# A transformer block on one core: gate and head stores issued by ScalarE, gate loads issued by POOL, and SiLU written as a product with Sigmoid

## The chip, the cores and the metric

The kernel runs on one core of a Trainium2 chip. The core's engines run their own instruction streams and wait for each other through semaphores: TensorE (PE in the profile; PEld are its weight loads), VectorE (DVE), ScalarE (ACT), GpSimd (POOL) and SyncE (SP, which only issues DMA transfers here). ScalarE and POOL can issue transfers too; each engine's instructions, its transfer issues among them, go in program order. The metric is the device time of one execution in microseconds, lower being better.

## The reference

One layer of a block over 512 latent tokens and 256 context tokens, D = 1024, all fp32. Cut to what the change touches:

```python
h_lat = rms_norm(x, norm_mix_g) * (1.0 + sc1) + sh1              # (512, 1024)
(qkv, ..., g_a, ..., g_b, m_a, m_b) = split_last(h_lat @ w_in, IN_SIZES)
# g_a, g_b: 512 wide (4 heads of 128); m_a, m_b: 1024 wide

def gated_head_norm(o, g, gate, dtype):                           # o: output of a scan, per head
    o = o * lax.rsqrt(jnp.mean(o * o, axis=-1, keepdims=True) + EPS) * g
    return (from_heads(o) * jax.nn.silu(gate)).astype(dtype)

ya = gated_head_norm(oa, gdn_g, g_a, dtype) @ w_up_a              # branch A: gated DeltaNet
yb = gated_head_norm(ob, hgrn_g, g_b, dtype) @ w_up_b             # branch B: HGRN2
mix = (jax.nn.sigmoid(m_a) * ya + jax.nn.sigmoid(m_b) * yb) @ w_out
x = x + g1 * mix
x = x + g2 * swiglu(rms_norm(x, norm_ffn_g) * (1.0 + sc2) + sh2, ffn_w_in, ffn_w_out)
out = rms_norm(x, final_norm_g)
```

## The kernel before

Activations lie transposed: 128 features on the partitions, 512 tokens along them. A matmul in fp32 precision is made of three: each operand is split into a high part (`hi`, a cast on ScalarE, L100) and a low part (`lo`, a subtraction on VectorE, L102), and `mm3` (L110) adds hi·hi, hi·lo and lo·hi. Weights come as `raw` tiles on SyncE's queue (L92).

The stages follow each other roughly so: modulation and norm of the input (to 60 us), the first gates (60 to 85 us), the projections and scans of the two branches (85 to 580 us), the join of both branches with their up-projections (580 to 645 us), the output projection, and the feed-forward part (from 690 us).

*Gates.* 24 rows of gate columns of `w_in`, each 128 x 512: numbers 0 to 3 are `g_a`, 4 to 7 `g_b`, 8 to 15 `m_a`, 16 to 23 `m_b`. `gate_out` copies one from PSUM (`pg` for the first six, `pgate` after) into a tile `gt` of a ring of two, and stores it to the scratch tensor `gdram` in DRAM. The first eight are 16 to 23, in that order; 0 to 15 are worked in as filler among the scans, the last ones just ahead of the join.

*Heads.* `head_norm` takes one head's scan output: squares (L427), a mean (L429 or L431 on VectorE), a power on POOL (L432), a scaling on ScalarE into `on` (L434), a transpose on TensorE into `pt` (L437), and a copy `y` (L438), which is stored to `ydram`. Names with `p0` to `p3` are pairs of DeltaNet heads' state, `h0` to `h3` HGRN2 heads.

*Join.* `branch(br)` loads for each of its four heads the gate `ug` and the head `uy` back from DRAM, makes SiLU of the gate, multiplies, and splits the product into `yh` and `yl`. `up(br, W, ys)` then makes eight up-projections `pup`, in two PSUM banks in turn; each is evicted by VectorE with its merge gate `mg`, on which ScalarE has made Sigmoid. For branch 0 the eviction writes into `mt`, a view of the tile `x1` (printed as `x`); for branch 1 it adds up.

*Modulation.* In the background POOL loads pieces of `mod_w` (`mwb`, L833, and `mwe`, L847), and VectorE sums them (`acc`, L835; L851 to L854).

The order of instructions on each engine is set by a scheduler, by priorities and estimated durations of its own. A table `PLAN` sets the order in which the scans' steps are written, a priority raised by 5000 puts the last gates and the modulation behind. The engine that issues a transfer is the one on whose `nc.` name it is called: `nc.sync`, `nc.scalar`, `nc.gpsimd`.

Of the kernel before, what the change touches and what calls it, by code (L numbers as in the profile page):

```python
# [7 lines left out]
F32 = mybir.dt.float32  # L8
F32R = mybir.dt.float32r
U8 = mybir.dt.uint8  # L10
AF = mybir.ActivationFunctionType
ALU = mybir.AluOpType

P = 128
# [3 lines left out]
SEQ = 512  # L18
# [30 lines left out]
def body(tc, T, out, tap=None):  # L49
    nc = tc.nc  # L50
# [7 lines left out]
    with ExitStack() as root:  # L58
# [17 lines left out]
        def bank(tag, name):  # L76
            return ps_.tile([P, 512], F32, name=name, tag=tag, bufs=BANKS[tag])

        def pmm(name):
            return bank("mm", name)  # L80
# [48 lines left out]
        gdram = dr.tile([24, P, SEQ], F32, name="gdram")  # L129
        ydram = dr.tile([8, P, SEQ], F32, name="ydram")  # L130
# [3 lines left out]
        def gate_out(i, ps, pool, tag="raw"):  # L134
            gt = pool.tile([P, SEQ], F32, name=f"gt{i}", tag=tag, bufs=2)
            nc.scalar.copy(gt[:, :], ps[:, :])
            nc.sync.dma_start(gdram[i, :, :], gt[:, :])

        def gate(i, pool, wpool=None, tag="mm"):
            gate_out(i, feat(split([W_IN[:, gcols[i]:gcols[i] + P]], KT, P, wpool), lat, SEQ, f"pgate{i}", tag=tag), pool, "gt")  # L140
# [18 lines left out]
        with ExitStack() as st:  # L159
# [172 lines left out]
            for i in range(NG0):  # L332
                gate_out(16 + i, pg0[i], sp, "gt")
# [90 lines left out]
        def head_norm(po, gcol, i, on, y, ss, tag, name, eq=None):  # L424

            for c in range(4):
                nc.scalar.activation(on[:, c, :], po[:, c, :], AF.Square, accum_out=ss[:, c:c + 1])  # L427
            if eq is None:
                nc.vector.tensor_scalar(ss, ss, 1.0 / P, EPS, op0=ALU.mult, op1=ALU.add)  # L429
            else:  # L430
                nc.vector.scalar_tensor_tensor(ss, ss, 1.0 / P, eq, op0=ALU.mult, op1=ALU.add)  # L431
            nc.gpsimd.tensor_tensor(ss, ss, mhalf[:, 0:4], op=ALU.pow)  # L432
            for c in range(4):
                nc.scalar.activation(on[:, c, :], po[:, c, :], AF.Copy, scale=ss[:, c:c + 1])  # L434
            pt = bank(tag, f"{name}_pt")
            for c in range(4):
                nc.tensor.transpose(pt[:, P * c:P * c + P], on[:, c, :], ident)  # L437
            nc.scalar.activation(y, pt[:, :], AF.Copy, scale=gcol)  # L438
            nc.sync.dma_start(ydram[i, :, :], y)

        def hgrn(h):

# [467 lines left out]
        for item in before.split():  # L910
            name, n = item.split(":")
# [26 lines left out]
        for item in after.split():  # L938
            name, n = item.split(":")
# [6 lines left out]
        with pool("yp", 1) as yp, pool("mg", 1) as mg:  # L946
            mt = view(x1, 0, ((SEQ, KT), (1, SEQ)))

            def branch(br):

                yh = yp.tile([P, NH, SEQ], F32R, name=f"yh{br}", tag=f"yh{br}")
                yl = yp.tile([P, NH, SEQ], F32R, name=f"yl{br}", tag=f"yl{br}")
                for h in range(NH):
                    gt = yp.tile([P, SEQ], F32, name=f"ug{br}{h}", tag="ug", bufs=4)
                    nc.sync.dma_start(gt[:, :], gdram[4 * br + h, :, :])
                    nc.scalar.activation(gt[:, :], gt[:, :], AF.Silu)
                    yt = yp.tile([P, SEQ], F32, name=f"uy{br}{h}", tag="uy", bufs=3)
                    nc.sync.dma_start(yt[:, :], ydram[4 * br + h, :, :])
                    nc.vector.tensor_tensor(yt[:, :], gt[:, :], yt[:, :], op=ALU.mult)
                    nc.scalar.copy(yh[:, h, :], yt[:, :])  # L960
                    nc.vector.tensor_tensor(yl[:, h, :], yt[:, :], yh[:, h, :].bitcast(F32), op=ALU.subtract)
                return yh, yl

            def up(br, W, ys):

                for j in range(0, KT, 2):
                    w = split([W[:, P * j:P * j + 2 * P]], 4, 2 * P)
                    for i in (j, j + 1):
                        ps = pmm(f"pup{br}{i}")
                        o = P * (i - j)  # L970
                        mm3(ps[:, :], [lambda k, t=t: t[:, k, o:o + P] for t in w], [lambda k, t=t: t[:, k, :] for t in ys], 4)
                        gt = yp.tile([P, SEQ], F32, name=f"mg{br}{i}", tag="ug", bufs=4)
                        nc.sync.dma_start(gt[:, :], gdram[8 + 8 * br + i, :, :])
                        nc.scalar.activation(gt[:, :], gt[:, :], AF.Sigmoid)
                        if br == 0:
                            nc.vector.tensor_tensor(mt[:, i, :], gt[:, :], ps[:, :], op=ALU.mult)
                        else:
                            nc.vector.tensor_tensor(gt[:, :], gt[:, :], ps[:, :], op=ALU.mult)
                            nc.vector.tensor_tensor(gt[:, :], mt[:, i, :], gt[:, :], op=ALU.add)
                            nc.scalar.copy(mh[:, i, :], gt[:, :])  # L980
                            nc.vector.tensor_tensor(ml[:, i, :], gt[:, :], mh[:, i, :].bitcast(F32), op=ALU.subtract)
                    yield
# [179 lines left out]
```

## Time and profile before

| | us |
|---|---|
| median of 3 runs | 1079.61 (1078.65 to 1081.12) |
| profiled execution, its own time | 1081.61 |
| profiled execution, its span | 1079.6 |
| TensorE busy in the span | 1014.1 |
| VectorE busy | 656.5 |
| ScalarE busy | 554.5 |
| POOL busy | 76.6 |

The span runs from the first to the last instruction of the profiled execution. TensorE's granted clock over it was 0.990 of full speed. In rows of the timeline the columns are: start, duration, engine, line of the kernel, operation, out<-in, shapes, count, and in brackets how long the engine had been idle and what released it. Tile names are shown there without their numbers. "q" after an engine's name means its sequencer issuing a transfer.

### The profile page before, as it was taken

The page shows a single profiled execution, that of the slowest core. Times are in us where ns is not written, and L with a number is a line of the kernel's source. Part 1 is how long each engine was busy: PE and PEld are TensorE (multiplying, and loading weights), DVE is VectorE, ACT ScalarE, POOL GpSimd, SP SyncE. Part 2 cuts the span into 40 slices and gives each one's busy share as a digit, 9 for nine tenths or more (in the row PEclk, how much of TensorE's full clock was granted, in tenths as well). Part 3 has the DMA queues.
Part 4 walks back from the last instruction along what each step waited for, and adds up shares of the span by engine and source line. Part 5 has one row for each costly group of instructions (what it writes and reads, how often), then busy time and mean ns, then how long its engine had stood idle before and what let it go on. Part 6 is the DMA issues. An engine that isn't in the chain of part 4 may idle for free.

```text
span 1079.6 us, 16501 instructions
## 1 busy us (share of the span) xinstructions
PE 1014.1 (94%) x6455; PEld 839.9 (78%) x6455; DVE 656.5 (61%) x1238; ACT 554.5 (51%) x1042; POOL 76.6 (7%) x133
## 2 busy tenths in 40 slices
PE   4999999979999999999999899999999999999996
PEld 2686788858897877789777688797888878888785
DVE  3336886789867967976797565776343433422524
ACT  3456578748976765887774643442222222221212
POOL 1010000320002022000201000010000000000000
PEclk8999999999999999999999999999999999999999
DMA  9953412122004213200738743455333323322222
GB/s 329 290 168 91 138 55 65 54 79 59 3 11 147 64 45 88 59 2 22 241 112 280 239 159 120 137 158 174 98 97 96 96 85 98 97 97 96 86 95 95
DMA packets 134529, 122.07 MB, mean 113 GB/s; under 512 B 5533, under 2 KB 110259, under 8 KB 134451
## 3 DMA queue, kind: packets, MB, share of 16 engines
q1 hardware_dynamic: 127715, 100.20, 29.9%
q0 software_dynamic: 4640, 17.30, 4.9%
q10 hardware_dynamic: 2096, 3.50, 0.9%
q8 instruction: 51, 0.84, 0.3%
q14 instruction: 27, 0.22, 0.1%
HBM read 110.51 MB, written 10.49 MB: 112 GB/s over the span
## 4 chain that ended last, share of the span: by engine, by line
PE 60%; DVE 13%; DMA 9%; ACT 7%; issue 7%; POOL 3%; SPq 0%; POOLq 0%; ACTq 0%; DVEq 0%
PE pf L110 20%; PE pfo L110 10%; PE pg L330 3%; PE pup L110 3%; PE h_z L110 3%; PE pgate L110 2%; DMA mwb<-in_mod_w_dram 2%; DVE lo L102 2%; DMA mwe<-in_mod_w_dram 2%; PE h_zv L110 2%; DMA ug<-gdram 1%; ACT hi L100 1%; DMA gdram<-gt 1%; PE p_s_pk L801 1%; PE g_k_zl L110 1%
## 5 line engine op out<-in xcount | busy, mean ns | idle before, releaser
L100 ACT CAST hi<-raw 128x1024 fp32r<-128x1024 f32 (+1 forms) x131 | 129.7, 991 | 279.9 <-PE pf L110 97.3
L102 DVE TENSOR_TENSOR lo<-raw,hi 128x1024 fp32r<-128x1024 f32 (+1 forms) x131 | 150.5, 1150 | 172.6 <-ACT hi L100 172.2
L110 PE MATMUL pf<-hhi,lo 128*128 128x512 f32 (+1 forms) x352 | 133.8, 380 | 0.8 <-DVE lo L102 0.8
L110 PE MATMUL pf<-hhi,hi 128*128 128x512 f32 (+1 forms) x352 | 133.8, 381 | 0.0
L110 PE MATMUL pf<-hlo,hi 128*128 128x512 f32 (+1 forms) x352 | 133.7, 380 | 0.0
L110 PEld LDWEIGHTS pf<-hhi,lo 128*128 128x128 f32 x352 | 66.2, 188 | 13.7 <-DVE lo L102 1.2
L110 PEld LDWEIGHTS pf<-hlo,hi 128*128 128x128 f32 x352 | 66.2, 188 | 12.5 <-DVE hlo L1042 0.2
L110 PEld LDWEIGHTS pf<-hhi,hi 128*128 128x128 f32 x352 | 66.1, 188 | 12.5
L110 PE MATMUL pfo<-lo,uh 128*128 128x512 f32 x176 | 68.8, 391 | 0.1
L110 PE MATMUL pfo<-hi,ul 128*128 128x512 f32 x176 | 68.5, 389 | 0.0
L110 PE MATMUL pfo<-hi,uh 128*128 128x512 f32 x176 | 67.9, 390 | 0.0
L110 PE MATMUL pgate<-hhi,lo 128*128 128x512 f32 x144 | 59.2, 412 | 6.5 <-DVE lo L102 6.5
L110 PE MATMUL pgate<-hhi,hi 128*128 128x512 f32 x144 | 59.2, 411 | 2.3 <-ACT hi L100 2.3
L110 PE MATMUL pgate<-hlo,hi 128*128 128x512 f32 x144 | 58.2, 404 | 0.0
L1098 DVE TENSOR_TENSOR sg<-sg,pf 128x512 f32<-128x512 f32 x22 | 15.1, 687 | 49.3 <-PE pf L110 49.3
L835 DVE SCALAR_TENSOR_TENSOR acc<-mwb,sc,acc 128x256 f32<-128x256 f32 x72 | 34.5, 484 | 12.4 <-DMA mwb<-in_mod_w_dram 11.2
L110 PEld LDWEIGHTS pfo<-lo,uh 128*128 128x128 f32 x176 | 33.0, 188 | 7.8 <-DVE lo L102 1.0
L110 PEld LDWEIGHTS pfo<-hi,uh 128*128 128x128 f32 x176 | 32.8, 188 | 7.4 <-ACT hi L100 0.7
L110 PEld LDWEIGHTS pgate<-hhi,lo 128*128 128x128 f32 x144 | 27.8, 193 | 13.8 <-DVE lo L102 8.9
L110 PE MATMUL h_z<-hhi,hi 128*128 128x512 f32 x96 | 38.1, 397 | 0.4 <-ACT abT L376 0.3
L110 PEld LDWEIGHTS pfo<-hi,ul 128*128 128x128 f32 x176 | 33.0, 188 | 6.8
L110 PE MATMUL h_z<-hhi,lo 128*128 128x512 f32 x96 | 38.0, 396 | 0.0
(443 smaller groups left out, 2498.3 us busy)
## 6 DMA issues: line engine op xcount, KB each, us to landing
raw<-in_ffn_w_in_dram SPq DMA_DIRECT2D x44, 512.0 KB, 3.7
raw<-in_w_in_dram SPq DMA_DIRECT2D x37, 512.0 KB, 3.7
raw<-in_ffn_w_out_dram SPq DMA_DIRECT2D x22, 512.0 KB, 3.6
mwb<-in_mod_w_dram POOLq DMA_DIRECT2D x18, 512.0 KB, 4.6
mw<-in_mod_w_dram SPq DMA_DIRECT2D x16, 512.0 KB, 6.0
mwe<-in_mod_w_dram POOLq DMA_DIRECT2D x7, 1024.0 KB, 6.1
gdram<-gt SPq DMA_DIRECT2D x24, 256.0 KB, 3.3
raw<-in_w_in_dram SPq DMA_DIRECT2D x18, 256.0 KB, 2.9
```

The source lines that it names most:

```text
L100: nc.scalar.copy(hi[:, :, :], raw[:, :, :])
L102: nc.vector.tensor_tensor(lo[:, :, :], raw[:, :, :], hi.bitcast(F32), op=ALU.subtract)
L110: nc.tensor.matmul(ps, a[u](k), b[v](k), start=(start and n == 0), stop=(stop and n == tot - 1))
L330: nc.tensor.matmul(pg0[i][:, :], u[:, P * i:P * i + P], v[:, d, :], start=(d == 0 and n == 0), stop=(d == KT - 1 and n == 2))
L801: nc.tensor.matmul(pk[:, 2 * P:3 * P], kend[:, :], u[:, :], start=True, stop=True)
L835: nc.vector.scalar_tensor_tensor(acc[:, :], mw[:, k - k0, :], sc[:, k:k + 1], acc[:, :], op0=ALU.mult, op1=ALU.add)
L1098: nc.vector.tensor_tensor(sg[:, :], sg[:, :], pgu[1][:, :], op=ALU.mult)
```

## The change

1. `gate_out` and `head_norm` issue their stores (24 and 8) on ScalarE's queue instead of SyncE's.
2. The loads of `ug` (8) and `mg` (16) are issued on POOL's queue instead of SyncE's. The loads of `uy` stay on SyncE's.
3. `ug * SiLU` is no longer one activation and one product. VectorE multiplies `uy` by the raw gate, ScalarE makes Sigmoid of the gate, and VectorE multiplies again. The sequence of activations needs two loads of activation tables where it needed five.
4. `mg` has a ring of four buffers of its own; it shared one of four with `ug`.

```diff
         def gate_out(i, ps, pool, tag="raw"):
             gt = pool.tile([P, SEQ], F32, name=f"gt{i}", tag=tag, bufs=2)
             nc.scalar.copy(gt[:, :], ps[:, :])
-            nc.sync.dma_start(gdram[i, :, :], gt[:, :])
+            nc.scalar.dma_start(gdram[i, :, :], gt[:, :])
...
             nc.scalar.activation(y, pt[:, :], AF.Copy, scale=gcol)
-            nc.sync.dma_start(ydram[i, :, :], y)
+            nc.scalar.dma_start(ydram[i, :, :], y)
...
                     gt = yp.tile([P, SEQ], F32, name=f"ug{br}{h}", tag="ug", bufs=4)
-                    nc.sync.dma_start(gt[:, :], gdram[4 * br + h, :, :])
-                    nc.scalar.activation(gt[:, :], gt[:, :], AF.Silu)
+                    nc.gpsimd.dma_start(gt[:, :], gdram[4 * br + h, :, :])
                     yt = yp.tile([P, SEQ], F32, name=f"uy{br}{h}", tag="uy", bufs=3)
                     nc.sync.dma_start(yt[:, :], ydram[4 * br + h, :, :])
+                    nc.vector.tensor_tensor(yt[:, :], gt[:, :], yt[:, :], op=ALU.mult)
+                    nc.scalar.activation(gt[:, :], gt[:, :], AF.Sigmoid)
                     nc.vector.tensor_tensor(yt[:, :], gt[:, :], yt[:, :], op=ALU.mult)
...
-                        gt = yp.tile([P, SEQ], F32, name=f"mg{br}{i}", tag="ug", bufs=4)
-                        nc.sync.dma_start(gt[:, :], gdram[8 + 8 * br + i, :, :])
+                        gt = yp.tile([P, SEQ], F32, name=f"mg{br}{i}", tag="mg", bufs=4)
+                        nc.gpsimd.dma_start(gt[:, :], gdram[8 + 8 * br + i, :, :])
                         nc.scalar.activation(gt[:, :], gt[:, :], AF.Sigmoid)
```

Lines of the changed kernel behind the products stand one further down: the eviction of branch 0 is L977 there, and the two products and the Sigmoid are L958, L960 and L959.

The scheduler moves instructions on every engine; SyncE has 181 instructions instead of 237, POOL 151 instead of 127. Four places follow, in the order in which each engine has its instructions.

ScalarE at the first gates, before:

```order
L136 COPY gt20_558<-pg0_4_214 128x512
L136 COPY gt21_561<-pg0_5_215 128x512
L136 COPY gt22_595<-pgate22_570 128x512
L100 CAST hi4_981<-raw4_979 128x1024
L301 ACTIVATE chi_75<-px10_632,mcol_189 128x256
L136 COPY gt23_629<-pgate23_604 128x512
L303 ACTIVATE hf10_636<-px10_632,mcol_189 128x256
```

and after:

```order
L136 COPY gt20_558<-pg0_4_214 128x512
L137 DMA gdram_77<-gt20_558 128x512
L136 COPY gt21_561<-pg0_5_215 128x512
L137 DMA gdram_77<-gt21_561 128x512
L136 COPY gt22_595<-pgate22_570 128x512
L137 DMA gdram_77<-gt22_595 128x512
L100 CAST hi4_981<-raw4_979 128x1024
L136 COPY gt23_629<-pgate23_604 128x512
L301 ACTIVATE chi_75<-px10_632,mcol_189 128x256
L137 DMA gdram_77<-gt23_629 128x512
L303 ACTIVATE hf10_636<-px10_632,mcol_189 128x256
```

Each store now stands behind its copy on the same engine, and the copy of gate 23 has moved ahead of the first piece of `chi`, the context's normed input.

POOL ahead of the join, before:

```order
L833 DMA mwb424_5579<-in_mod_w_dram 128x4x256
L432 TENSOR_TENSOR h2_ss_6117<-h2_ss_6117,mhalf_102 128x4
L833 DMA mwb430_5587<-in_mod_w_dram 128x4x256
L833 DMA mwb434_5593<-in_mod_w_dram 128x4x256
L1028 TENSOR_TENSOR st2_5454<-st2_5454,mhalf_102 128x1 x4
```

and after:

```order
L833 DMA mwb424_5579<-in_mod_w_dram 128x4x256
L833 DMA mwb430_5587<-in_mod_w_dram 128x4x256
L955 DMA ug00_6150<-gdram_77 128x512
L833 DMA mwb434_5593<-in_mod_w_dram 128x4x256
L955 DMA ug01_6159<-gdram_77 128x512
L955 DMA ug02_6168<-gdram_77 128x512
L955 DMA ug03_6177<-gdram_77 128x512
L974 DMA mg00_6205<-gdram_77 128x512
L974 DMA mg01_6222<-gdram_77 128x512
```

The second gate load stands behind the last modulation load of this stage, `mwb434`.

VectorE at the first eviction of an up-projection, before (branch 1's heads are `uy10` to `uy13`):

```order
L961 TENSOR_TENSOR yl1_6223<-uy11_6235,yh1_6222 128x512
L959 TENSOR_TENSOR uy12_6243<-ug12_6240,uy12_6243 128x512
L976 TENSOR_TENSOR x1_5451<-mg00_6201,pup00_6188 128x512
L959 TENSOR_TENSOR uy13_6251<-ug13_6248,uy13_6251 128x512
L961 TENSOR_TENSOR yl1_6223<-uy12_6243,yh1_6222 128x512
L961 TENSOR_TENSOR yl1_6223<-uy13_6251,yh1_6222 128x512
L976 TENSOR_TENSOR x1_5451<-mg01_6218,pup01_6205 128x512
```

and after:

```order
L958 TENSOR_TENSOR uy11_6239<-ug11_6237,uy11_6239 128x512
L960 TENSOR_TENSOR uy11_6239<-ug11_6237,uy11_6239 128x512
L977 TENSOR_TENSOR x1_5451<-mg00_6205,pup00_6192 128x512
L958 TENSOR_TENSOR uy12_6248<-ug12_6246,uy12_6248 128x512
L962 TENSOR_TENSOR yl1_6227<-uy11_6239,yh1_6226 128x512
L958 TENSOR_TENSOR uy13_6257<-ug13_6255,uy13_6257 128x512
L977 TENSOR_TENSOR x1_5451<-mg01_6222,pup01_6209 128x512
```

The first eviction has moved ahead of branch 1's third head, and the second ahead of the third head's second product.

VectorE at the second head norm of pair p2 (`mwe31` and `mwe32` are pieces of the modulation), before:

```order
L853 SCALAR_TENSOR_TENSOR mwe31_4897<-mwe31_4897,sc_173 128x256 x6
L431 SCALAR_TENSOR_TENSOR p2_hs1_4879<-p2_hs1_4879,g3_vec_3500 128x4
L854 TENSOR_TENSOR mwe31_4897<-mwe31_4897 128x256
L851 TENSOR_SCALAR mwe32_5355<-mwe32_5355,sc_173 128x256 x2
```

and after:

```order
L853 SCALAR_TENSOR_TENSOR mwe31_4897<-mwe31_4897,sc_173 128x256 x6
L854 TENSOR_TENSOR mwe31_4897<-mwe31_4897 128x256
L851 TENSOR_SCALAR mwe32_5355<-mwe32_5355,sc_173 128x256 x2
L862 TENSOR_TENSOR vc_169<-pmo31_4908,vc_169 128x2
L431 SCALAR_TENSOR_TENSOR p2_hs1_4879<-p2_hs1_4879,g3_vec_3500 128x4
```

The mean of the head's squares has moved behind the end of one piece of the modulation, the beginning of the next, and L862, which takes column sums (`pmo31`) that TensorE makes of the first piece.

## The prediction

> **What bounds the kernel now.** I read the page first: span, busy times, and the chain of work that ended last.
>
> ```profile
> span 1079.6 us, 16501 instructions
> PE 1014.1 (94%) x6455; PEld 839.9 (78%) x6455; DVE 656.5 (61%) x1238; ACT 554.5 (51%) x1042; POOL 76.6 (7%) x133
> PE 60%; DVE 13%; DMA 9%; ACT 7%; issue 7%; POOL 3%; SPq 0%; POOLq 0%; ACTq 0%; DVEq 0%
> ```
>
> The reader is to see TensorE busy 94% of the time, and the change takes no matmul away. It can gain only from TensorE's idle time, 1079.6 - 1014.1 = 65.5 us, and only where a gate, a head or a branch load ends a wait. SyncE's queue, which the change empties most, has 0% of the chain: a shorter SyncE queue by itself brings nothing. Next comes the list of TensorE's waits (columns: total us, times, longest), of which four can be reached by the edited lines.
>
> ```profile
> PE pup L110 <- DVE x L976: 3.6, 2, 2.3
> PE p_pt L437 <- ACT p_on L434: 2.9, 2, 1.9
> PE pab L375 <- ACT gt L136: 1.3, 1, 1.3
> PE pab L375 <- ACT chi L301: 1.0, 1, 1.0
> ```
>
> Together they hold 8.8 us, so the change cannot gain much more. The other waits are touched only by the new order of the program.
>
> **The join of branches and up-projection.** The timeline of 600 to 617 us, by engine:
>
> ```profile
> 600.07 0.39 PE L110 MATMUL pup<-yh,hi 128*128 128x512 f32 x1
> 607.93 0.50 PE L110 MATMUL pup<-yh,hi 128*128 128x512 f32 x1 [2.26 <-DVE x L976]
> 612.34 0.50 PE L110 MATMUL pup<-yh,hi 128*128 128x512 f32 x1 [1.35 <-DVE x L976]
> 616.24 0.50 PE L110 MATMUL pup<-yh,lo 128*128 128x512 f32 x1 [0.42 <-DVE lo L102]
> 600.48 1.28 ACT L956 ACT_TABLE_LOAD   x1 [0.69 <-DMA ug<-gdram]
> 611.53 1.28 ACT L974 ACT_TABLE_LOAD   x1 [0.58 <-DMA mg<-gdram]
> 606.59 0.69 DVE L959 TENSOR_TENSOR uy<-ug,uy 128x512 f32<-128x512 f32 x1 [1.48 <-ACT ug L956]
> 607.20 0.68 DVE L976 TENSOR_TENSOR x<-mg,pup 128x512 f32<-128x512 f32 x1
> 611.60 0.68 DVE L976 TENSOR_TENSOR x<-mg,pup 128x512 f32<-128x512 f32 x1
> ```
>
> Two PSUM banks take turns, and an up-projection is 12 matmuls. The third one (607.93) needs the first evicted, which began at 607.20 on VectorE, though the first was computed long before. That eviction stood behind the product of branch 1's third head, which waited for its SiLU. So TensorE lost 2.26 + 1.35 + 0.42 = 4.03 us.
>
> In the new order the first eviction stands behind branch 1's second head instead, and since all activations here are Sigmoid, neither of the two table loads shown comes between. Estimate: the last gate ends when the first up-projection begins (600.07), its copy (0.59, row below) and store (0.33, below) leave ScalarE by about 601.3, the second head's Sigmoid, as long as a product (0.69), ends at 602.0, the product at 602.7, the eviction at 603.4. The third up-projection wants its bank at 607.93 - 2.26 = 605.67, so about 2 us are spare. I leave 0.3 us for the second eviction and the weights: **-3.7 us**, bounds -4.0 and 0.
>
> What the join gets in return is eight VectorE products (8 x 0.69 = 5.5 us) and gate loads on POOL's queue:
>
> ```profile
> 580.00:600.00 20.00, 20.00 (x90) 16.57 (x89) 13.48 (x22) 12.02 (x18) 0.75 (x1) 1.00 0.89 287
> 581.56 0.75 POOL L833 DMA_DIRECT2D mwb<-in_mod_w_dram  x1 [4.17 <-DVE acc L835]
> 584.15 0.44 SPq L955 DMA_DIRECT2D ug<-gdram  x1
> 592.63 1.22 DVE L102 TENSOR_TENSOR lo<-raw,hi 128x1024 fp32r<-128x1024 f32 x1
> ug<-gdram SPq DMA_DIRECT2D x8, 256.0 KB, 4.6
> mwb<-in_mod_w_dram POOLq DMA_DIRECT2D x18, 512.0 KB, 4.6
> ```
>
> The first line is one stretch of the table by stretches (stretch, length, busy us of TensorE, its weight loads, VectorE, ScalarE, POOL, then clock and DMA). VectorE was busy 13.5 of 20 us, so 5.5 us more fit. On POOL the second gate load now stands behind the last modulation load, issued at 581.56, and so leaves about 582.3, before its old slot on SyncE at 584.15. It lands about 582.3 + 4.6 = 586.9. Its product stands in VectorE ahead of the split of the last gate's weights (592.63), which TensorE needs 24 matmuls before 600.07, at 594.6 (24 x 0.227 us, by 12 matmuls in 2.72 between the first two up-projections). So 5.7 us lie between landing and split: loads on POOL cost nothing while they are less than that late.
>
> **The first gates.** ScalarE copies gates 16 to 23 out of PSUM through two buffers, so a copy waits until the store two gates earlier has landed. From the chain, and from the list of DMA issues (median us from issue to landing at the end):
>
> ```profile
> 78.25 0.59 ACT gt L136
> 78.86 0.32 SPq L137
> 79.29 0.38 SPq L92
> 79.72 4.43 DMA gdram<-gt
> 84.22 0.59 ACT gt L136
> gdram<-gt SPq DMA_DIRECT2D x24, 256.0 KB, 3.3
> out_dram<-x SPq DMA_DIRECT2D x4, 256.0 KB, 2.3
> out_dram<-x ACTq DMA_DIRECT2D x4, 256.0 KB, 2.1
> ```
>
> The store that ends the wait could have left at 78.86 and left at 79.72, behind a weight load on SyncE. On ScalarE's own queue that hold of 0.86 goes and one issue (0.43, worked out below) comes: **-0.4 us**. Bounds: -2.3, if both waits of TensorE there (1.3 and 1.0) go, and +0.9, two issues with no hold gained. The far end needs stores that land sooner on ScalarE's queue; the two rows of the same output store, 2.1 against 2.3, give only 0.2 a store. In the Trainium skill, "DMA: Bandwidth & Descriptors", section "Issuing engines are not separate DMA queues" says that transfers started by different engines run interleaved on the same 16 DMA engines, and that spreading them saves only the time to start them. By that rule the term is the hold alone and the total -4.0; with landing as fast as 2.1 it would be the far end and the total -5.9.
>
> **The second head norm of pair p2.** Timeline at 521 us:
>
> ```profile
> 521.09 0.16 DVE L431 SCALAR_TENSOR_TENSOR p_hs<-p_hs,g_vec 128x4 f32<-128x4 f32 x1
> 521.21 0.42 DVE L854 TENSOR_TENSOR mwe<-mwe 128x256 f32<-128x256 f32 x1
> 521.55 0.61 DVE L851 TENSOR_SCALAR mwe<-mwe,sc 128x256 f32<-128x256 f32 x2
> 522.56 1.28 ACT L434 ACTIVATE p_on<-p_oa,p_hs 128x128 f32<-128x128 f32 x4 [2.27 <-POOL p_hs L432]
> 523.01 0.62 PE L437 MATMUL p_pt<-sq,p_on 128*128 128x128 f32 x2 [1.90 <-ACT p_on L434]
> ```
>
> The y store (L439) now lies on ScalarE between the two heads, and the new order puts more matmuls ahead of this transpose, which covers most of the 1.90 us. Against that, VectorE's L431 now stands behind L854 and the two L851, some 0.42 + 0.61 = 1.0 us later. It also stands behind L862, which waits for TensorE's column sums of that same piece, a short detour through TensorE that I count in the bounds. I take -1.6 + 1.0 = **-0.6 us**, bounds -1.9 and +1.0.
>
> **Stores on ScalarE elsewhere.** 24 further stores (16 gates, 8 heads) are issued by ScalarE:
>
> ```profile
> 69.46 1.08 ACT L136 COPY gt<-pg 128x512 f32<-128x512 f32 x2 [1.89 <-PE pg L330]
> 677.35 0.63 ACT L1019 ACTIVATE xt<-x 128x512 f32<-128x512 f32 x1 [1.10 <-DVE x L1018]
> 677.40 0.33 ACTq L1015 DMA_DIRECT2D xr<-in_x_dram  x1
> 480.00:540.00 60.00, 57.80 (x412) 51.08 (x412) 40.84 (x110) 44.39 (x115) 7.36 (x8) 1.00 0.38 120
> ```
>
> An issue takes 0.33 and there ran beside an activation, so the low price is 0. At most it adds the issue and the overlap lost between neighbours (two copies in 1.08 instead of 2 x 0.59, 0.10): 0.43, together 24 x 0.43 = 10.3 us. Of that I put ScalarE's share of the chain, 7%, on the path: **+0.7 us**. At worst it is ScalarE's busy share in a full stretch of the scans, 44.39 of 60, 74%: +7.6 us. I stay near the low end because only few of TensorE's waits in the list end with ScalarE. SyncE's 56 fewer instructions and the buffers of "mg"'s own cost nothing: neither stands in any engine's way. Three table loads fewer take 3 x 1.28 = 3.8 us off ScalarE; the two that TensorE felt are in the join's term.
>
> **Sum.** -3.7 - 0.4 - 0.6 + 0.7 = -4.0 us. The profiled execution took 1081.61 (its span 1079.6, and 2.0 around it), and so would take 1077.6. It is 2.0 over the median of the runs, 1079.61; against that median the forecast is **1075.6 us**.
>
> **Rivals.** First, slower: ScalarE's stores cost full price where ScalarE carries the scans. Place: 120 to 600 us; price 7.6 instead of 0.7, so -4.7 + 7.6 = +2.9, 1082.5 us. It ends above the old time once 4.7 / 10.3, or 46%, of their time is on the path. For it speaks the 74%; against it the chain's 7%.
>
> Second, the loads on POOL come late and the join waits as long as before under another name: the join term is 0, the sum -0.3, 1079.3 us. From 5.7 us of lateness on, the last gate's weights wait too. Against it: POOL's 512 KB loads land in 4.6 us, as SyncE's 256 KB do, with VectorE busy 61%. The Trainium skill, "SBUF — State Buffer", "The DVE blocks DMA trap (SWDGE)", says that a transfer issued from POOL has its descriptors written by POOL, which is shut out while VectorE runs certain two-port operations. By that rule this rival would be the likely one; the 4.6 us speak against it.
>
> Third, what is won is given back, or the new order of the scans opens other waits like the transposes' (1.9 us each): one takes the forecast to 1077.5, two to 1079.4, four to 1083.2. Against a loss right behind the join speaks this stretch, in which TensorE has no idle time to fill:
>
> ```profile
> 640.00:660.00 20.00, 20.00 (x90) 16.57 (x89) 15.11 (x21) 9.54 (x13) 0.00 (x0) 1.00 0.43 142
> ```
>
> Fourth, the stores land sooner and the far end of the first gates holds: 1073.7.
>
> **How the numbers follow.** Less than 0.2% (2.2 us) can't be told from no change here: faster is under 1077.4, slower over 1081.8. Forecast 0.52 (its own range 1072.5 to 1077.4), ScalarE's price 0.12, late POOL 0.16, given back 0.14 (0.08 same, 0.06 slower), stores sooner 0.06. Faster 0.52 + 0.06 = 0.58, same 0.16 + 0.08 = 0.24, slower 0.12 + 0.06 = 0.18. The range, 1070.5 to 1082.0, takes in all but most of ScalarE's price and the outer ends of the bounds.
>
> **What the new profile would show.** Right: no TensorE wait above 0.5 us between the first and fourth up-projection; two table loads in all; ScalarE's copy of gate 23 starting 0.4 to 0.9 us sooner after gate 16's. Wrong: waits of TensorE on ScalarE's gt, p_on, hi or scan tiles that were not in the list (first rival); VectorE's products at the join waiting for ug or mg transfers (second); the join closed but idle time of TensorE elsewhere larger than 62 us (third).

## The result: 1.1% slower, and the profile after

| | before | after |
|---|---|---|
| median (us) | 1080.36 (4 runs, 1078.65 to 1081.62) | 1091.33 (4 runs, 1090.45 to 1094.25) |
| ratio after / before | | 1.0109 [1.009, 1.0128] |
| profiled execution, span | 1079.6 | 1089.1 |
| TensorE busy in it | 1014.1 | 1017.3 |
| span less TensorE busy | 65.5 | 71.8 |

The forecast was 1075.6, four below the time before; the time is eleven above the time before, and outside the range (1070.5 to 1082.0). Busy times and chain, from the page of after:

```profile
span 1089.1 us, 16493 instructions
PE 1017.3 (93%) x6455; PEld 840.1 (77%) x6455; DVE 661.1 (61%) x1246; ACT 550.7 (51%) x1039; POOL 86.9 (8%) x157
PE 63%; DVE 14%; DMA 8%; ACT 7%; issue 5%; POOL 2%; SPq 0%; POOLq 0%; ACTq 0%; DVEq 0%
```

The span grew by 9.5 us: 6.3 us more of TensorE's idle time, and 3.2 us more in which the same 6455 matmuls were busy. No new engine became the bound. ScalarE, which took over 32 stores, is busy 4 us less than before and has the same 7% of the chain. The idle time has new names, in the list of TensorE's waits of after (total us, times, longest):

```profile
PE h__pt L437 <- ACT h_on L434: 3.3, 4, 1.8
PE pab L375 <- ACT chi L301: 3.3, 1, 3.3
PE h_pA L488 <- DVE h_kq L513: 2.8, 2, 1.6
PE pgate L110 <- ACT hi L100: 2.8, 3, 1.8
PE g_v_zl L110 <- DVE lo L102: 2.3, 1, 2.3
PE h_pA L488 <- ACT h_kqd L501: 2.0, 1, 2.0
```

The evictions that held up the up-projections are no longer in it. Nor are two further waits of before that the prediction had not shown, the first two rows here; the third, at the last head's transposes, grew (timeline of before, then the same place in after):

```profile
338.73 0.33 PE L437 MATMUL p_pt<-sq,p_on 128*128 128x128 f32 x1 [1.00 <-ACT p_on L434]
416.95 0.50 PE L110 MATMUL pgate<-hhi,lo 128*128 128x512 f32 x1 [1.49 <-DVE lo L102]
577.09 0.33 PE L437 MATMUL h__pt<-sq,h_on 128*128 128x128 f32 x1 [1.11 <-ACT h_on L434]
```

```profile
588.85 0.33 PE L437 MATMUL h__pt<-sq,h_on 128*128 128x128 f32 x1 [1.76 <-ACT h_on L434]
```

So waits went and others came, and more came than went. Four of the places, in the order of the program.

**First gates.** ScalarE (and TensorE in the last row), timeline of after:

```profile
79.82 0.59 ACT L136 COPY gt<-pg 128x512 f32<-128x512 f32 x1 [0.41 <-ACT gt L136]
83.27 0.59 ACT L136 COPY gt<-pgate 128x512 f32<-128x512 f32 x1 [2.86 <-DMA gdram<-gt]
85.28 0.58 ACT L136 COPY gt<-pgate 128x512 f32<-128x512 f32 x1
85.75 0.57 ACT L301 ACTIVATE chi<-px,mcol 128x256 fp32r<-128x256 f32 x1
86.38 0.42 PE L375 MATMUL pab<-chi,wab 128*32 128x256 f32 x1 [3.26 <-ACT chi L301]
```

The copy of gate 22 waits 2.86 us for a store to land. Behind it on ScalarE stand a cast, the copy of gate 23 and only then `chi`, which TensorE needs. It waits 3.26 us; before, two waits there had 1.28 + 1.02 = 2.30.

**A weight split behind the modulation, at 335 us.** VectorE and TensorE:

```profile
335.21 0.62 DVE L851 TENSOR_SCALAR mwe<-mwe,sc 128x256 f32<-128x256 f32 x2 [3.77 <-DMA mwe<-in_mod_w_dram]
338.12 1.22 DVE L102 TENSOR_TENSOR lo<-raw,hi 128x1024 fp32r<-128x1024 f32 x1
339.39 0.50 PE L110 MATMUL g_v_zl<-hhi,lo 128*128 128x512 f32 x1 [2.33 <-DVE lo L102]
```

VectorE stands still for 3.77 us for a load of the modulation that nobody needs yet. The split of the weights stands behind the sums of that load.

**The second head norm of pair p2:**

```profile
533.87 0.62 DVE L851 TENSOR_SCALAR mwe<-mwe,sc 128x256 f32<-128x256 f32 x2 [1.57 <-DMA mwe<-in_mod_w_dram]
534.47 0.15 DVE L431 SCALAR_TENSOR_TENSOR p_hs<-p_hs,g_vec 128x4 f32<-128x4 f32 x1
536.40 0.33 PE L437 MATMUL p_pt<-sq,p_on 128*128 128x128 f32 x1 [1.65 <-ACT p_on L434]
```

L431 stands behind the next piece of the modulation and its load, as the order tables showed. TensorE waits 1.65 us instead of 1.90.

**The join:**

```profile
595.58 0.75 POOL L833 DMA_DIRECT2D mwb<-in_mod_w_dram  x1 [0.78 <-DVE acc L835]
596.33 1.62 POOL L955 DMA_DIRECT2D ug<-gdram  x3
600.41 1.00 DVE L835 SCALAR_TENSOR_TENSOR acc<-mwb,sc,acc 128x256 f32<-128x256 f32 x2 [3.21 <-DMA mwb<-in_mod_w_dram]
601.31 1.28 ACT L959 ACT_TABLE_LOAD   x1 [4.89 <-DMA ug<-gdram]
603.61 1.05 ACT L100 CAST hi<-raw 128x1024 fp32r<-128x1024 f32 x1
604.10 1.00 DVE L835 SCALAR_TENSOR_TENSOR acc<-mwb,sc,acc 128x256 f32<-128x256 f32 x2 [1.17 <-DMA mwb<-in_mod_w_dram]
607.02 1.22 DVE L102 TENSOR_TENSOR lo<-raw,hi 128x1024 fp32r<-128x1024 f32 x1
608.29 0.50 PE L110 MATMUL pgate<-hhi,lo 128*128 128x512 f32 x1 [1.88 <-DVE lo L102]
616.36 0.50 PE L110 MATMUL pup<-yh,hi 128*128 128x512 f32 x1 [0.52 <-ACT yh L961]
626.79 0.47 PE L110 MATMUL pup<-yh,hi 128*128 128x512 f32 x1 [0.52 <-ACT mg L975]
```

The 4.03 us of waits among the up-projections shrank to two of 0.52 (and one of 0.22). But VectorE waits for the last two loads of the modulation (3.21 and 1.17 us), and behind their sums stands the split of the last gate's weights: 1.88 us of TensorE are given back. The cast ahead of that split is late too. On ScalarE it stands behind the first Sigmoid, whose table load waited 4.89 us for a gate load on POOL's queue, and it ends at 603.61 + 1.05 = 604.66; VectorE's sums and products hold the split for another 2.4 us. The last of the modulation loads left POOL at 595.58 and was summed from 604.10 on, 8.5 us later; in the whole run such a load lands in 4.6. From 593 us on, POOL issues the last modulation loads and the first gate loads nearly at once, and these transfers were slow, on ScalarE's queue too (DMA issues of after, 570 to 606 us alone, median us to landing at the end):

```profile
ug<-gdram POOLq DMA_DIRECT2D x4, 256.0 KB, 8.4
gdram<-gt ACTq DMA_DIRECT2D x3, 256.0 KB, 7.9
mg<-gdram POOLq DMA_DIRECT2D x3, 256.0 KB, 8.7
```

In the whole run these three medians are 5.3, 2.8 and 3.1. The core's transfers moved 316 GB/s from 590 to 600 us and 395 from 600 to 606, against 287 from 580 to 600 in before.

**The clock.** TensorE's busy time times its granted clock is nearly the same in both profiles, 1014.1 x 0.990 = 1004.0 and 1017.3 x 0.988 = 1005.1 (one step in the clock's last digit is worth 1 us): the 3.2 us of busy time are clock, as closely as that can be told. Stretches of 10 us (columns as in the prediction), first two of after, then the same two of before:

```profile
360.00:370.00 10.00, 7.31 (x59) 5.14 (x58) 8.91 (x15) 7.32 (x14) 0.22 (x4) 0.83 0.35 100
450.00:460.00 10.00, 7.99 (x48) 7.31 (x47) 8.59 (x22) 6.07 (x12) 0.16 (x1) 0.83 0.39 107
```

```profile
360.00:370.00 10.00, 10.00 (x56) 8.64 (x56) 9.72 (x16) 6.85 (x10) 0.00 (x0) 1.00 0.28 80
450.00:460.00 10.00, 8.51 (x95) 7.03 (x94) 8.81 (x14) 7.47 (x15) 0.91 (x2) 1.00 0.20 54
```

In these stretches of after lie waits of 1.78 us (`pgate`, on the weights' high part) and 2.02 us (`h_pA`, on `h_kqd`). The clock of 0.83 costs another 0.17 x 10 = 1.7 us each.

### The profile page after: what moved, and what is told of

It reads as the page before. It is cut to its first block, busy times and chain, and to the rows that moved or that the text cites. A ratio compares the mean times of both kernels' runs of the same rounds, so it can differ in the third digit from the quotient of the medians.

```text
span 1089.1 us, 16493 instructions
## 1 busy us (share of the span) xinstructions
PE 1017.3 (93%) x6455; PEld 840.1 (77%) x6455; DVE 661.1 (61%) x1246; ACT 550.7 (51%) x1039; POOL 86.9 (8%) x157
## 4 chain that ended last, share of the span: by engine, by line
PE 63%; DVE 14%; DMA 8%; ACT 7%; issue 5%; POOL 2%; SPq 0%; POOLq 0%; ACTq 0%; DVEq 0%
PE pf L110 22%; PE pfo L110 10%; PE pg L330 3%; PE pgate L110 3%; PE pup L110 3%; DVE lo L102 2%; DMA mwe<-in_mod_w_dram 2%; PE h_z L110 2%; PE h_pA L488 2%; DMA mwb<-in_mod_w_dram 1%; PE p_pD L664 1%; PE g_k_zl L110 1%; PE p_s_pk L792 1%; DVE p_Z L696 1%; ACT hi L100 1%
## 5 line engine op out<-in xcount | busy, mean ns | idle before, releaser
L110 PEld LDWEIGHTS pf<-hhi,hi 128*128 128x128 f32 x352 | 66.1, 188 | 12.5
```

The lines of the kernel that those rows point to most:

```text
L110: nc.tensor.matmul(ps, a[u](k), b[v](k), start=(start and n == 0), stop=(stop and n == tot - 1))
```

## The experiments

Two theories stood against each other at the start. One (A in the expectations): the stores cost ScalarE time that the path needs (the prediction's first rival). The other (B): each edit is cheap where it stands, but the edits make the scheduler choose another order for the whole program, and that order waits more (its third rival). A further one (C) put the loss down to POOL's loads and the join. Each ratio below is to the kernel before, run on the same chip.

To separate an edit from the order it causes, some kernels have their order fixed. At the end of the program, edges of issue order alone, with no wait in them, tie each instruction to the one that is to stand ahead of it on its engine:

```diff
+        pin(tc, ORDER)    # for each engine, a list of its instructions
...
+            if last is not None:
+                tc.add_manual_dep(i, last, mb.DependencyInfo(mb.DependencyClass.NoSync, mb.DependencyReason.DATA), reason="pin")
```

| run | ratio [95%] | TensorE idle in its profile | mean granted clock (runs) |
|---|---|---|---|
| after | 1.0109 [1.009, 1.0128] | 71.8 | 0.987 (4) |
| e1 | 1.0125 [1.0092, 1.0158] | 73.8 | 0.983 (6) |
| e2 | 1.0054 [1.0032, 1.0076] | 67.2 | 0.986 (12) |
| e3 | 1.0005 [0.9981, 1.0028] | 64.8 | 0.990 (12) |
| e4 | 1.0094 [1.0057, 1.013] | 73.0 | 0.985 (7) |
| e5 | 1.0069 [1.0046, 1.0092] | 67.2 | 0.987 (6) |
| e6 | 1.0164 [1.0142, 1.0186] | 69.8 | 0.980 (4) |
| e7 | 1.0058 [1.0036, 1.0081] | 66.1 | 0.990 (6) |
| e8 | 1.0146 [1.0121, 1.017] | 70.7 | 0.983 (5) |
| e9 | 1.0045 [1.0029, 1.0062] | 67.0 | 0.989 (7) |
| e10 | 1.0068 [1.0051, 1.0085] | 66.4 | 0.987 (6) |
| e11 | 1.0066 [1.004, 1.0091] | 66.8 | 0.985 (7) |
| e12 | 0.9981 [0.9958, 1.0004] | 62.0 | 0.989 (12) |
| e13 | 1.0014 [0.9991, 1.0036] | 64.6 | 0.987 (12) |
| e14 | 0.9965 [0.9945, 0.9986] | 63.1 | 0.990 (12) |

Idle is the span less TensorE's busy time, 65.5 for before; before's clock in the runs beside them was 0.990 to 0.991.

### Which part: e1, e2

e1 is the kernel before with the stores alone moved, in the order that the scheduler then makes:

```diff
-            nc.sync.dma_start(gdram[i, :, :], gt[:, :])
+            nc.scalar.dma_start(gdram[i, :, :], gt[:, :])
...
-            nc.sync.dma_start(ydram[i, :, :], y)
+            nc.scalar.dma_start(ydram[i, :, :], y)
```

> Before's kernel with the 32 stores (L137, L439) on ScalarE's queue and nothing else changed; the scheduler orders it anew. Theory A, ScalarE pays about 0.4 us for each store in the scans and TensorE waits for it: +9 to +12 us against before. Theory B, the new order that the scheduler makes is to blame, not the issues: also +5 to +12, since the order changes here too. Theory C, the loads on POOL and the join are to blame: within 2 us of before.

e2 is after with these two lines as in before: loads on POOL, Sigmoid and the ring of `mg` remain.

> The changed kernel with its stores back on SyncE's queue: loads on POOL, Sigmoid, mg's own buffers remain. Theory A and B: about 3 us faster than before (the join's gain of the changed kernel alone), or what a third order makes of it. Theory C: as slow as the changed kernel, +9 to +12 us.

The stores alone cost as much as the whole change: 1.0125. Their waits are those of after, from the list of e1:

```profile
PE h__pt L437 <- ACT h_on L434: 3.8, 4, 2.2
PE pab L375 <- ACT chi L301: 3.6, 1, 3.6
PE g_v_zl L110 <- DVE lo L102: 2.5, 1, 2.5
```

Theory C falls with e1, which has neither loads on POOL nor Sigmoid. e2 leaves the scans as they were (the last head's transposes begin at 576.77 us, 0.3 earlier than in before) and loses some 5 us later, at the join. Little of that is waiting: TensorE waits 1.69 and 1.28 us for the last gates' weights and 1.89 for an eviction, 4.9 us against 4.0 in before. But its granted clock is 0.86, 0.80 and 0.83 in the three stretches of 10 us from 590 us on, and there it was 1.00 in before: (0.14 + 0.20 + 0.17) x 10 = 5.1 us. So e2 too is slower, but by less than e1. That points to the stores, but not yet to how: e1's waits end on VectorE as well as on ScalarE, which issues the stores.

### The engine or the order: e3, e4

e3 is e1 with the order of before fixed on every engine; each store is still issued by ScalarE, behind its copy or at most two instructions later.

> The stores on ScalarE's queue, but every engine keeps before's order of instructions; only the 32 stores are added to ScalarE, each directly behind its copy or at most two instructions later. Theory A: as slow as the stores alone, +9 to +12 us. Theory B: within 2 us of before, 32 issues at 0.4 us on a ScalarE that is half idle.

e4 is the other half: the order of after fixed on every engine, the stores issued by SyncE.

> The changed kernel's order on every engine, but the 32 stores are issued by SyncE, so ScalarE issues none of them. Theory A: about 3 us faster than before. Theory B: nearly as slow as the changed kernel, +6 to +11 us against before.

The two lists of waits, e3's first:

```profile
PE p_pt L437 <- ACT p_on L434: 3.2, 2, 2.6
PE pup L110 <- DVE x L976: 2.4, 2, 1.4
PE pab L375 <- ACT chi L301: 1.7, 1, 1.7
PE pab L375 <- ACT gt L136: 0.2, 1, 0.2
```

```profile
PE pab L375 <- ACT chi L301: 3.7, 1, 3.7
PE h__pt L437 <- ACT h_on L434: 3.3, 4, 1.8
PE g_v_zl L110 <- DVE lo L102: 2.2, 1, 2.2
```

All 32 stores on ScalarE, in before's order: no difference that can be measured, and of after's new waits only the one on `chi`, half as long. After's order with the stores back on SyncE: 1.0094, and the waits of after one by one. e1 and e3 differ in the order alone, after and e4 in the engine of the stores alone: the order costs the time; ScalarE's issuing does not. The first rival falls with e3, and the third stands. No run has POOL's loads and Sigmoid with before's order throughout. That they are not the cause is argued from e1, which has neither and loses as much.

### Where in the program: e5, e7, e8

All three are the whole change, with a mixed order. e7 has before's order as far as the transposes of the head h1 (about 405 us), then after's. e8 has after's to that point, before's to the transposes of h2 (about 576 us), then after's. e5 has before's order to the transposes of h2, then after's.

> The whole change; before's order up to the transposes of head h1 (about 405 us), the changed kernel's order from there. The trace of the changed kernel has lost 5 us by there and 6 us more up to the join. If losses by order are local: slower than before by 4 to 7 us. If one early misplacement makes everything late: as before, within 2 us.

> The whole change; the changed kernel's order up to the transposes of head h1 (about 405 us), then before's order to the last head's transposes, then the changed kernel's for the join. If losses are local: slower than before by 3 to 6 us. If the loss of the first half is caught up later (slack ahead of the join): within 2 us of before.

> The whole change, but every engine keeps before's order up to the last head's transposes (about 576 us) and takes the changed kernel's order from there. If the order of the scans is the cause: the scans cost what they cost before (0 to +1 us for the stores), the first gates save 0.7, the join saves 1 to 4, so 1 to 4 us faster than before. If loads on POOL or stores on ScalarE hurt whatever the order: 2 to 10 us slower than before.

e8 and e5 differ by the order ahead of 405 us alone: 0.8%. e7 and e5 differ by the order from 405 to 576 us: nothing that can be told (1.0058 and 1.0069). From 576 us on all three have after's order. e5 loses 0.7%, and in its profile 5.6 of the 8.1 us come after that point (the last head's transposes begin at 579.58 us, 2.5 later than in before). 0.8 and 0.7 add up to more than the whole change lost (1.1%), though the intervals of e8 and of after overlap.

e7 came out as expected, 5.8 us slower than before. The other two did not. e8 lost 15 us instead of 3 to 6. e5 was to be 1 to 4 us faster if the order of the scans were the cause; it is 7 us slower, which is the side of its rival. So the order of the scans is not the whole loss: some of it arises at the join, by after's order there, by the transfers or by the seam. In e5 the idle time is only 1.7 us above before's, and TensorE is busy 1020.5 us against 1014.1: most of its loss is clock. At the seam between two orders VectorE also stands still for work that the other order would have placed there (8.46 us in e5, ahead of the split at 586.47), so how much of each part belongs to the change and how much to the seam stays open.

### The last gates and the join: e9, e10, e11

e9 has e5's order, with all loads and stores of the change back on SyncE; Sigmoid and the ring of `mg` stay. e10 is e5 with the last gate's copy and weights ahead of the first head's Sigmoid on ScalarE, and their split ahead of the last sums of the modulation on VectorE. e11 is e9 with those moves.

> Before's order up to the last head's transposes, the changed kernel's order for the join, Sigmoid and mg's own buffers kept, but all loads and stores on SyncE's queue; against the run with the whole change in the same order it takes POOL and ScalarE out of the transfers. If POOL's queue is what holds the join up (gate loads behind modulation loads that wait for VectorE): the waits of TensorE for the last gate's weights (3.5 and 1.2 us) go and the join's gain of 4 us stays, 1 to 4 us faster than before. If the order within the join does it, or the burst of loads: waits for those weights stay above 2 us, 4 to 8 us slower than before.

> The whole change with before's order of the scans; in the join the copy of gate 13 and the cast of the last gate's weights stand ahead of the first Sigmoid of a branch gate on ScalarE, and their split ahead of the last modulation load's sums on VectorE. If ScalarE standing at the late gate load is what holds the weights up: 4 to 7 us faster than with the same scan order and the join unmended, so within 2 us of before. If the wait moves on to the next late thing: within 2 us of the unmended one, 5 to 9 us slower than before.

> The two together: loads and stores on SyncE's queue, before's order of the scans, the join's mended order, Sigmoid and mg's own buffers. It is the version that the readings so far point to: 2 to 4 us faster than before (the join's 4 us without its new waits). If the join's gain is not to be had: within 2 us of before or slower.

None of them comes back to before. In e9 TensorE waits 0.98 and 3.43 us for the last gates' weights, in e10 2.62, in e11 1.40, and e10 and e11 then wait 1.75 and 2.44 us for the low parts of the heads at the up-projections. With the loads on SyncE a loss at the join is there too, so POOL's queue isn't its only cause. e9 came out on the side of "the order within the join, or the burst of loads", e10 on the side of the wait that moves on; e11 was to be 2 to 4 us faster and is 6 slower. What POOL and ScalarE add can't be told: the intervals of e5 and e9 overlap. What the three share is after's order at the join, the Sigmoid form with its eight further products, and the seam. Neither the Sigmoid form nor the seam is needed for the wait: e1 has SiLU, its gate loads on SyncE and one order throughout, and waits 3.07 us for the last gate's weights.

### Single moves on the new order: e6

After, with three splits behind which TensorE waited (2.33 us at 337, 1.78 at 361, 1.88 at 606) moved ahead of what delayed them:

```diff
 VectorE
+lo37 (weights, ahead of the sums of mwe30)
 ...
 ScalarE, VectorE
+hi27, lo27 (weights, some instructions earlier)
 ...
+gt13, hi52 (ahead of the first head's Sigmoid), lo52 (ahead of the sums of mwb434)
```

> The changed kernel with its own order but for three places where a weight split stood behind a waiting instruction: the split of weights 37 ahead of the modulation sum that waits for its load; the cast and split of weights 27 ahead of a conv step that waits; the cast and split of the last gate's weights 52 ahead of the first SiLU product and of the last modulation load's sums. If such in-order queueing is how the new order costs time: the three waits of TensorE (2.3, 1.8, 1.9 us) go, and the slow-clock stretches behind them, 4 to 8 us faster than the changed kernel. If the loss is only shifted to the next late thing: within 2 us of the changed kernel.

By the two ratios it is 0.55% slower than after itself, worse than either expectation. The waits moved: 2.34 us at 342 us, 2.60 us at 617 us, and this one, beside the stretch that follows it:

```profile
370.14 2.04 PE L488 MATMUL h_pA<-h_kq 128*128 128x128 f32 x8 [3.59 <-ACT g_q_pad L611]
```

```profile
370.00:380.00 10.00, 9.23 (x60) 7.83 (x61) 7.15 (x12) 5.83 (x11) 0.22 (x4) 0.51 0.37 109
```

Idle time fell by 2.0 us against after, and busy time rose by 7.5: about half speed over ten microseconds is 0.49 x 10 = 4.9 us of that, more than the moves had saved. On this order, lifting three instructions made others late.

### The join alone: e13, e12, e14

These keep before's order, stores, loads and SiLU. e13 moves two instructions:

```diff
 VectorE
+x1<-mg00,pup00          (eviction of the first up-projection)
 uy12<-ug12,uy12         (product of branch 1's third head)
-x1<-mg00,pup00
+x1<-mg01,pup01
 uy13<-ug13,uy13
 ...
-x1<-mg01,pup01
```

> The kernel before with its order on every engine; only the evictions of up-projections 0 and 1 stand on VectorE ahead of the products of branch 1's third and fourth heads. The merge gates still share a ring with the head gates, so mg02 still loads only after those products. Theory (order and buffers are both needed): the waits 2.26 and 1.35 go, but the third up-projection's eviction still waits for mg02's Sigmoid, which ended at 613.4, so TensorE waits some 2.5 to 3.3 us at the fifth up-projection instead; 0 to 1.5 us faster than before. Rival (the place of the evictions is enough): 3 to 4 us faster.

The waits of 2.26 and 1.35 us went. At the fifth up-projection this came, with another 0.53 behind it:

```profile
612.75 0.50 PE L110 MATMUL pup<-yh,hi 128*128 128x512 f32 x1 [1.59 <-ACT hi L100]
```

That is ScalarE, still occupied with the Sigmoids of `mg02` and `mg03` that came late. 4.03 became 2.12 us, somewhat less than the theory gave it, and no difference in time can be measured.

e12 adds what keeps ScalarE free for that:

```diff
-                        gt = yp.tile([P, SEQ], F32, name=f"mg{br}{i}", tag="ug", bufs=4)
+                        gt = yp.tile([P, SEQ], F32, name=f"mg{br}{i}", tag="mg", bufs=4)
 SyncE:   mg02 and mg03 loaded behind mg01
 ScalarE: Sigmoids of mg02 and mg03, and hi58 (the third weights), ahead of branch 1's last cast
 VectorE: pup00, pup01 and pup02 evicted earlier, lo58 ahead of branch 1's last split
```

> The kernel before with the order of before on every engine, apart from the join: mg has a ring of four buffers of its own, the loads of mg02 and mg03 follow mg01's on SyncE, VectorE evicts up-projections 0, 1 and 2 ahead of the product or split they stood behind, and ScalarE makes the Sigmoids of mg02 and mg03 and the high part of the weights 58 one cast earlier. Stores, loads and SiLU stay as before. Theory (the join's 4.03 us are a matter of order and buffers there, and what the change lost lies in the new order of the scans): 3 to 4 us faster than before, 1076.5 to 1077.5 against 1080.4, the waits of TensorE on evictions of the first four up-projections under 0.6 us together, all waits up to 590 us as in before. Rival (what ends the join's wait makes another one there, as in every kernel so far): the waits return at the fifth or sixth up-projection or at the last gate, and the time is within 1.5 us of before.

Two loads of `xr` that ScalarE issues at 603.98 and 605.95 us in before also come later, after 620 us, in e12 and e14. Of the three waits in before's join one is left, 1.30 us where the theory had under 0.6, and nothing came at the fifth up-projection:

```profile
607.45 0.68 DVE L976 TENSOR_TENSOR x<-mg,pup 128x512 f32<-128x512 f32 x1
608.18 0.50 PE L110 MATMUL pup<-yh,hi 128*128 128x512 f32 x1 [1.30 <-DVE x L976]
```

The span of its profile is 3.3 us shorter. The ratio, 0.9981, is on the side of a gain, with the upper end of its interval at 1.0004: it fits the theory in the trace but doesn't show it in time.

e14 moves the first eviction further, ahead of branch 1's first head, and L431 of the second head of p2 between the sums of `mwe31`:

```diff
 VectorE
+x1<-mg00,pup00
 uy10<-ug10,uy10
 ...
 mwe31 (L853) x2
+p2_hs1 (L431)
 mwe31 (L853) x4
-p2_hs1 (L431)
```

> As e12 (the kernel before and its order, with the join alone reordered and a ring of four for mg), with two more moves on VectorE. The first eviction (pup00) stands ahead of the product of branch 1's first head; in e12 it stood behind two products and two splits and began at 607.45, and VectorE was idle for 5.69 us ahead of them. L431 of the second head of pair p2 stands after two of the six L853 of mwe31 instead of after all six. Theory (single moves in place pay where nothing else is reordered): TensorE's wait of 1.30 on that eviction goes, and the 1.90 us at that head's transposes shrink to 0.5 or less; some 2.5 us less than e12, 1074 to 1077. Rival (slower granted clock or a wait right behind takes it back): within 1 us of e12.

```profile
519.84 0.62 PE L437 MATMUL p_pt<-sq,p_on 128*128 128x128 f32 x2 [0.31 <-ACT p_on L434]
606.12 0.50 PE L110 MATMUL pup<-yh,hi 128*128 128x512 f32 x1 [0.92 <-DVE x L976]
```

The head's wait went from 1.90 to 0.31, the join's from 4.03 to 0.92. The time is 1078.05 against 1082.52 on that chip, 0.9965 [0.9945, 0.9986]: some 0.35% faster than before, and the only kernel here whose whole interval lies on that side. The interval of its gain, 1.5 to 6.0 us, holds what these waits lost (1.59 + 3.11 = 4.7 us). Its idle time fell by less, 2.4 us: in this profile the feed-forward part waited 2.7 us for weights (`pf` on `lo`), 1.9 more than before. The interval overlaps with e12's, so the last two moves' own gain isn't shown.

## Why the prediction was wrong

The step that failed is a sentence behind the list of waits: "The other waits are touched only by the new order of the program." The prediction priced that order as a rival with a chance of 0.14, by counting waits "like the transposes'", and put its own sum at four places only. The runs showed in its place that the order is nearly all of the loss: 1.0094 for after's order without the stores on ScalarE (e4), of 1.0109 for the whole; 1.0005 for the stores in before's order (e3). Point by point:

- **Bound.** Right that only TensorE's idle time can be gained. That this time can also grow, and that the granted clock falls with it, stood nowhere in the sum: 6.3 us of idle time and 3.2 us of clock.
- **The join, -3.7.** The mechanism was right: the evictions no longer hold up the up-projections, and e14 gets 3.1 us there by order and buffers alone. The working on POOL failed at both terms of "it lands about 582.3 + 4.6". The second gate load left at 596.33, 14.0 us later, because the modulation load ahead of it waited for VectorE's sums. The weights were wanted later as well, at 608.29 - 1.88 = 606.4 instead of 594.6; that leaves it 2.2 us late. And the gate loads took 8.4 us, 3.8 more. The two make 6.0 us, and the working had 5.7 to spare. The second rival had said that late loads would make the last gate's weights wait, and they did (1.88). But it had looked at the gates' loads alone; VectorE's split stood behind sums that waited for the modulation's own, nearly twice as slow in the same crowd (8.5 us against 4.6). Net, from the rows: -4.03 + 0.52 + 0.22 + 0.52 + 1.88 = -0.9.
- **The first gates, -0.4.** The sign was wrong: 3.26 for 2.30, +1.0, just over the upper bound (+0.9). For the edit alone the size came true, by luck: in e3, with before's order, the two waits add to 1.9 instead of 2.3. The hold had been misread. What left at 78.86 was gate 20's store; gate 21's copy ran from there to 79.45, so its store, which left at 79.72, was held for 0.27 us and not for 0.86, and 0.43 for an issue would have made the term +0.2. In e3 `chi` comes later, behind gate 22's copy, which waits 1.81 us for a store (TensorE: 1.68 for 1.02), and gate 23's copy no longer waits for one (0.17 for 1.28). From e3 to after, `chi` starts 1.6 us later, counted from gate 16's copy: 1.1 because gate 22's copy waits 2.86 us for a store instead of 1.81, and 0.5 because `chi` stands behind the copy of gate 23, which the order tables ahead of the prediction show and the working left without a price. By the rule of the Trainium skill ("DMA: Bandwidth & Descriptors", "Issuing engines are not separate DMA queues") only the time to start a store would be saved; e3 doesn't test it, since its eight stores here also landed in 3.4 us (median) instead of 3.9.
- **The second head norm, -0.6.** 1.90 became 1.65, and TensorE waited another 1.05 ahead of that piece's column sums (`pmo`): +0.8, within the bounds. L431 came not "some 1.0 us later" but at 534.47, after the load for which the next L851 waited 1.57 us. A move past instructions was costed by their durations, not by what they wait for. The single move of e14 shows what was to be had: 1.59 us.
- **Stores elsewhere, +0.7.** The price was right: after a store ScalarE's next copy begins 0.41 us later than it could (row at 79.82), against 0.43. On the path nothing of it is seen: e3 is between 2.1 us faster and 3.0 us slower than before. The first rival's 7.6 us are refuted. One reason given for the low price doesn't hold, though: that "only few of TensorE's waits in the list end with ScalarE". In the whole list of before 19 of the 34 lines do, 21.5 of 55.7 us.
- **Signs named ahead.** Right: no wait of TensorE from the second to the fourth up-projection (0.52 and 0.22 within the first), and two table loads. Gate 23's copy came later, not sooner (85.28 - 70.32 = 14.96 us after gate 16's, against 84.22 - 69.46 = 14.76). The third sign of failure, "the join closed but idle time of TensorE elsewhere larger than 62 us", is what happened: 71.8 in all. The sign of the first rival showed too (2.0 us on `h_kqd`, 1.8 on `hi`), although e3 refutes that rival: the two signs didn't tell these rivals apart.

What decided the scheduler in favour of these places stays open. Nor is it shown which of after's waits costs how much; the mixed orders place some 0.8% ahead of 405 us, no closer.

## What to carry to other kernels

Where a scheduler sets the order, giving an instruction to another engine can reorder the whole program, as here: pin the old order first and measure the edit, then the order. Walk the difference of the two orders over the whole program, and price each step past an instruction by what that instruction waits for. On an order that is otherwise good, moving the one instruction that stands in the way can be enough (e14, two waits); on the new order three such moves made the kernel slower (e6).

## What the runs showed of the hardware

**A short wait can cost twice.** In or right after stretches with single waits of 1.6 to 3.6 us the granted clock often fell to about 0.83 over 10 us, in e6 to 0.51. Over 2 us it reads 0.50 (after, 456 to 458 us), which is half speed. TensorE's busy time grows by about as much: times the clock it stays between 1003 and 1008 us in all profiles (e4: 1023.0 x 0.981 = 1003.6; e6: 1024.8 x 0.979 = 1003.3). The Trainium skill, "TensorE: Matmul & The Clock Gate", section "What's actually happening", says that TensorE's clock is halved after an idle window of about 3.4 us and comes back after as long a busy one. A clock of 0.83 is 3.4 us at half speed in 10, which agrees; but the waits ahead of it were as short as 1.59 us (e13, 0.83 from 610 to 620 us). Nor was each wait followed by it: after 2.33 us at 339 us the clock stayed at 1.00 in after, and the same wait of 1.59 us on `h_kq` stands beside 0.83 in e7 (560 to 570 us) and beside 1.00 in after (570 to 580).

**The clock goes along with the spread of the runs.** e12's twelve runs lie between 1073.71 us at a clock of 0.992 and 1086.87 at 0.982. Their spans times their clocks lie between 1063.3 and 1068.8, a range of 5.5 us instead of 13.3. That is the best case: from time to product the standard deviation falls from 3.7 to 1.5 us in e12, but only from 2.4 to 2.2 in the 23 runs of before beside it, and in e1's six runs it rises from 1.7 to 4.3. The mean of the product is 1069.0 for these 23 runs and 1065.3 for e12, 3.7 us less, with a mean clock of 0.9903 and 0.9885. This product was formed after the runs, so it is a hint of e12's gain and doesn't show it.

**Transfers issued in one stretch were slow, whichever engine issued them.** In the crowd ahead of the join a 256 KB transfer took 8 to 9 us from ScalarE's queue as from POOL's, and 5.8 (`uy`) from SyncE's; in e9, with the gate loads on SyncE, `mg` took 9.2 us in the same place (575 to 600 us). That agrees with the Trainium skill's section on issuing engines, named above. Its rule on POOL's descriptors ("SBUF — State Buffer", "The DVE blocks DMA trap (SWDGE)"), by which loads on POOL would suffer more than others, isn't seen: ScalarE's stores were as slow there, and over the whole run `mg` landed in 3.1 us, against 3.8 on SyncE before, and `ug` in 5.3 against 4.6.
